# Attention scores that multiply over 128 rows, and token-major products 512 columns wide

## The chip, the core and the metric

The kernel is one program on one core of a Trainium2 chip. The metric is device microseconds of the whole launch; each figure of record is the median of several runs. All data are float32; the program is written in Python for a framework that schedules each engine's queue itself. TensorE does the matrix products, ScalarE and VectorE what lies between them, GpSimd a few elementwise steps, SyncE issues most DMAs.

## What is computed

The reference is three layers on 256 tokens of width 1024. A first block mixes a chunked retention (8 heads) with a gated linear recurrence, and two layers of a second block follow, each with a second sequence of 256 context tokens beside the 256 of x. In such a layer one input projection feeds three branches (an mLSTM, an attention with 8 query and 2 key heads called gqa, an attention with a neighbourhood window and a bias called na); their outputs are projected, gated by sigmoids, summed and multiplied by an output matrix; a feed-forward part with a small convolution closes the layer. Cut to what the change touches:

```python
def attend(q, k, v):                       # gqa, the context tokens
    s = jnp.einsum('bqkgd,bskd->bkgqs', q, k).astype(jnp.float32) * (HEAD_DIM ** -0.5)
    p = jax.nn.softmax(s, axis=-1).astype(v.dtype)
    return jnp.einsum('bkgqs,bskd->bqkgd', p, v)
...
(mq, mk, mv, mo, mg, aq, ak, av, nq, nk, nv, zg) = jnp.split(h @ w_in[l], IN_SPLITS_2, axis=-1)
...
o = merge_branches(y_ml, y_ga, y_na, zg, w_branch[l], w_out[l])
x = x + ga1 * rms_norm_2(o, g_post_mix[l])
f = conv_ffn(modulate(rms_norm_2(x, g_pre_ffn[l]), sh2, sc2), w_up[l], conv_w[l], conv_b[l], w_down[l])
```

The heads of gqa and na are 64 wide. The second layer computes its branches for x alone (its context tokens are needed only as keys and values).

## The kernel before

**Two parts of every operand.** A float32 number goes to TensorE as two float32r parts, high and low. A weight chunk of 128 rows and 1024 columns is loaded (SyncE's queue, four buffers), its high part is a cast on ScalarE (L106), its low part a subtraction on VectorE (L107), or on GpSimd where the call says so. Every product of two such operands is three matmuls: high by high, high by low, low by high (`mm3`, L123 to L125).

**Two forms of product.** Feature-major (`gemm_pieces`, `gemm_feat`): the weights are the stationary operand, 128 by 128, and 256 or 512 tokens move. Token-major (`gemm_tok`, L147): 128 tokens of the activations are stationary and 256 columns of the weights move; both token tiles of a sequence share one PSUM bank of 512 columns, so a call for one sequence holds one bank and a call for two holds two. There are four such banks, named psg in the profile, handed out in turn. A chunk holds four k-tiles of 256 columns. Token-major are the values of the retention (`w_v`), the output projection of the first block (`w_out`), in each layer the queries of gqa (`w_aq`), its keys and values (`w_akv`), the values of mLSTM and na (`w_mv`, `w_nv`), the gate of mLSTM (`w_mo`), the output projection (`w_o`) and the down-projection (`w_dn`, 22 k-tiles). The last two go through `out_proj` (L1129): groups of 256 columns for both sequences, then the last groups for x, the chain of residual and norms of x, and the last groups for the context beside that chain. `take` (L1092) empties a bank: a square with a sum on ScalarE (L1097) and a product with a gate row on VectorE (L1098).

**Scores.** In gqa a query tile holds the high part of a head in rows 0 to 63 and the low part in rows 64 to 127. The keys are kept twice: `akh` has the high part in both halves, so one matmul over 128 rows gives (high + low) of the query by the high part of the key; `akl` has the low part in rows 0 to 63 alone, and a second matmul over 64 rows adds high by low (L838). It writes 256 keys at a time: four matmuls for the 512 keys of x, two for the 256 of the context. na does the same with `nkh` and `nkl`, 512 keys at a time for x (L925); its low parts are made on VectorE (L897) from the bank in which the projection lies.

**Order of the work.** `attend` (L629) walks over units (one head and 128 queries, or one head and two times 128 queries of the context): scores of unit i, then a stretch of other TensorE work that the code calls fillers, then P by V of the pair that closed, then the transposes of unit i-2. Softmax runs meanwhile on VectorE and ScalarE (L657 to L661). The fillers are pieces of the sigmoid gates, of the branch projections and of the conditioning; in gqa a fixed amount is traced with each unit (`FILLS`), in na what is left is spread over the units left. Per layer: 16 units of x in gqa and in na, and in the first layer 8 of the context in each.

## Time and profile before

| | |
|---|---|
| runs | 1889.11, 1892.03, 1887.61 us; median 1889.11 |
| profiled execution: span | 1885.2 us, 31900 instructions |
| its own launch time | not recorded apart from the three runs; the span stands 3.9 us under their median |
| TensorE (matmuls) | busy 1816.7 us, 96% |
| VectorE / ScalarE / GpSimd | 1152.7 / 861.4 / 252.9 us |
| mean granted TensorE clock | 0.987 |

A matmul's end in the profile is modelled and neighbours overlap, so the length of one is not what it costs. What it costs is the step from its start to the start of the next one, which is read in the timeline. "PE" are the matmuls, "PEld" the loads of the stationary operand that run beside them, "DVE" is VectorE, "ACT" ScalarE, "POOL" GpSimd. A form such as 64*128 64x256 says: 64 rows of the array by 128 columns, and 256 moving columns. Clock 1.00 is the upper of TensorE's two levels (2.4 GHz), 0.5 the lower (1.2 GHz).

### The profile page before, as it was taken

The numbers are of one execution on the slowest core, as the hardware profiler recorded it, in microseconds if no ns is written. First come the engines' busy times: TensorE is split into PE (matmuls) and PEld (weight loads), VectorE is DVE, ScalarE is ACT, GpSimd is POOL, SyncE is SP. The second block draws the span as 40 slices with busy tenths as digits, with TensorE's granted clock in tenths as the row PEclk, the third lists the DMA queues.
The fourth block names the chain that finished last, engine by engine and source line by source line (L and its number), as shares of the span: only waits on it lengthen the run. The fifth ranks groups of instructions, "written<-read, shape, count | busy, mean of one in ns | idle before, by whom it ended". The sixth has DMA issues, their size and how long they took to land.

```text
span 1885.2 us, 31900 instructions
## 1 busy us (share of the span) xinstructions
PE 1816.7 (96%) x12484; PEld 1595.4 (85%) x12484; DVE 1152.7 (61%) x2280; ACT 861.4 (46%) x1620; POOL 252.9 (13%) x182
## 2 busy tenths in 40 slices
PE   7998988999999999998999999998999999999998
PEld 6897987666898977787877889998889998779998
DVE  7878768444434667556655564239654448768874
ACT  5463344334435544434444443235555545446653
POOL 2214052000101021004111110021001011002210
PEclk9998998999999999999999999999999999999999
DMA  8853443555524342374354233344444744676563
GB/s 301 282 195 113 138 167 106 184 182 176 193 92 149 88 126 84 101 249 165 113 178 157 96 103 112 107 136 161 151 140 134 239 129 132 196 248 212 185 209 120
DMA packets 114422, 299.33 MB, mean 159 GB/s; under 512 B 28480, under 2 KB 41088, under 8 KB 114016
## 3 DMA queue, kind: packets, MB, share of 16 engines
q1 hardware_dynamic: 113568, 296.37, 47.9%
q8 instruction: 98, 1.61, 0.3%
q0 software_dynamic: 272, 0.36, 0.1%
q10 hardware_dynamic: 432, 0.57, 0.1%
q14 instruction: 52, 0.43, 0.1%
HBM read 281.46 MB, written 19.46 MB: 160 GB/s over the span
## 4 chain that ended last, share of the span: by engine, by line
PE 76%; DVE 6%; ACT 1%; issue 1%; DMA 0%; POOL 0%; DVEq 0%; ACTq 0%; POOLq 0%
PE psg L123 21%; PE psg L124 21%; PE psg L125 20%; PE pss L838 2%; PE psg L692 2%; PE psg L339 2%; PE pst L678 2%; PE pss L925 2%; PE pst L1054 1%; DVE wl L107 1%; PE pss L1042 1%; DVE rstd L240 1%; PE pst L264 0%; ACT wh L106 0%; DVE p L755 0%
## 5 line engine op out<-in xcount | busy, mean ns | idle before, releaser
L107 DVE TENSOR_TENSOR wl<-wr,wh 128x1024 fp32r<-128x1024 f32 x335 | 411.9, 1232 | 328.3 <-ACT wh L106 320.1
L106 ACT CAST wh<-wr 128x1024 fp32r<-128x1024 f32 x370 | 382.4, 1036 | 428.7 <-PE psg L124 182.9
L123 PE MATMUL psg<-hh,wh 128*128 128x256 f32 (+1 forms) x1712 | 577.0, 338 | 0.5 <-ACT hh L279 0.5
L124 PE MATMUL psg<-hl,wh 128*128 128x256 f32 (+1 forms) x1712 | 566.1, 331 | 0.0
L125 PE MATMUL psg<-hh,wl 128*128 128x256 f32 (+1 forms) x1712 | 564.4, 330 | 0.0
L123 PEld LDWEIGHTS psg<-hh,wh 128*128 128x128 f32 x1712 | 327.4, 192 | 54.1 <-issue 16.4
L125 PEld LDWEIGHTS psg<-hh,wl 128*128 128x128 f32 x1712 | 327.8, 192 | 30.2 <-issue 0.8
L124 PEld LDWEIGHTS psg<-hl,wh 128*128 128x128 f32 x1712 | 327.9, 192 | 25.8 <-issue 0.2
L123 PE MATMUL psg<-wh,hh 128*128 128x256 f32 x576 | 165.8, 288 | 6.2 <-DVE p L743 4.3
L125 PE MATMUL psg<-wh,hl 128*128 128x256 f32 x576 | 165.3, 287 | 2.4 <-DVE hl L283 2.4
L124 PE MATMUL psg<-wl,hh 128*128 128x256 f32 x576 | 164.8, 286 | 0.0
L123 PE MATMUL psg<-wh,midh 128*128 128x256 f32 x496 | 140.9, 284 | 0.0
L124 PE MATMUL psg<-wl,midh 128*128 128x256 f32 x496 | 140.9, 284 | 0.0
L125 PE MATMUL psg<-wh,midl 128*128 128x256 f32 x496 | 140.6, 284 | 0.0
L107 POOL TENSOR_TENSOR wl<-wr,wh 128x1024 fp32r<-128x1024 f32 (+1 forms) x35 | 82.5, 2368 | 373.4 <-ACT wh L106 373.4
L1283 POOL TENSOR_TENSOR u<-u 128x512 f32<-128x512 f32 (+1 forms) x44 | 63.3, 1439 | 410.3 <-DVE u L1239 405.3
L123 PEld LDWEIGHTS psg<-wh,hh 128*128 128x128 f32 x576 | 112.1, 195 | 7.1 <-DVE p L743 4.6
L125 PEld LDWEIGHTS psg<-wh,hl 128*128 128x128 f32 x576 | 111.9, 194 | 3.2 <-DVE hl L283 3.2
L124 PEld LDWEIGHTS psg<-wl,hh 128*128 128x128 f32 x576 | 112.0, 195 | 0.1
L123 PEld LDWEIGHTS psg<-wh,midh 128*128 128x128 f32 x496 | 95.6, 193 | 0.0
L124 PEld LDWEIGHTS psg<-wl,midh 128*128 128x128 f32 x496 | 95.6, 193 | 0.0
L125 PEld LDWEIGHTS psg<-wh,midl 128*128 128x128 f32 x496 | 95.6, 193 | 0.0
(300 smaller groups left out, 2915.4 us busy)
## 6 DMA issues: line engine op xcount, KB each, us to landing
wr<-in_w_up_dram SPq DMA_DIRECT2D x88, 512.0 KB, 3.4
wr<-in_w_mod_dram SPq DMA_DIRECT2D x55, 512.0 KB, 3.2
wr<-in_w_zg_dram SPq DMA_DIRECT2D x48, 512.0 KB, 3.5
wr<-in_w_dn_dram SPq DMA_DIRECT2D x45, 512.0 KB, 3.6
wr<-in_w_in_dram SPq DMA_DIRECT2D x40, 512.0 KB, 4.3
wr<-in_w_br_dram SPq DMA_DIRECT2D x24, 512.0 KB, 3.3
wr<-in_w_o_dram SPq DMA_DIRECT2D x20, 512.0 KB, 5.1
stock<-in_w_mod_dram SPq DMA_DIRECT2D x19, 512.0 KB, 6.5
```

The lines of the kernel that those rows point to most:

```text
L106: nc.scalar.copy(hi, raw)
L107: self.last_lo = (eng or nc.vector).tensor_tensor(lo, raw, hi.bitcast(F32), ALU.subtract).ins
L123: mm(ps, a[0], b[0], start=first, stop=False)
L124: mm(ps, a[0], b[1], start=False, stop=False)
L125: mm(ps, a[1], b[0], start=False, stop=last)
L240: nc.vector.scalar_tensor_tensor(w[:, c], t[:, c], t[:, c], v[:, c], ALU.mult, ALU.mult)
L339: nc.tensor.matmul(ps[32 * j : 32 * j + 32, 0:T], self.cv[:, kt], raw[j], start=kt == 0, stop=kt == KT - 1)
L678: nc.tensor.transpose(pt[:, k * P : (k + 1) * P], t[:, k * P : (k + 1) * P], self.idn)
L692: nc.tensor.matmul(po[64 * j : 64 * j + 64, :T], p[2](j, k), pTs[id(p), j][:, k], start=k == 0, stop=k == nk - 1)
L838: nc.tensor.matmul(ps[:, i * T : (i + 1) * T], qT[s, pr][: 64 * (2 - c), j, qt * P : (qt + 1) * P], kT[ss, kv][c], start=c == 0, stop=c == 1)
L925: nc.tensor.matmul(ps[:, :n], q[j][: 64 * (2 - c), s * T + qt * P : s * T + (qt + 1) * P], kk[j][c][:, ks], start=c == 0, stop=c == 1)
L1283: nc.gpsimd.tensor_tensor(a, a, b, ALU.mult)
```

## The change

Two edits in one.

Scores: the low parts of the keys are written into both halves, like the high parts, so the second matmul also runs over 128 rows; it adds the product of both low parts, which the kernel before leaves out. In gqa all 512 keys lie in one tile `akT`, and a unit of x takes two matmuls of 512 columns in place of four of 256.

Products: a new `gemm_wide` takes 512 weight columns at a time, one PSUM bank for each token tile (two banks for one sequence, four for two), two k-tiles a chunk. Before it starts, the piece of other work that is under way is finished. It replaces `gemm_tok` for all token-major products but `w_akv` and the second half of the down-projection's columns. What empties the banks now does it by token tile, 512 columns at a time.

```diff
+    def gemm_wide(self, src, x, seqs, order=None, eng=None, at=None):
+        while self.cur:
+            self.step()
+        pss = {s: [self.bank("g", 4) for _ in range(2)] for s in seqs}
+        nk = src.shape[-1] // 512
+        order = order or list(range(0, nk, 2))
+        for i, k0 in enumerate(order):
+            if at and i in at:
+                at[i]()
+            hi, lo = (a.rearrange("p (k c) -> p k c", c=512) for a in self.weights(src[:, k0 * 512 : (k0 + 2) * 512], eng))
+            for s in seqs:
+                for t in range(2):
+                    for j in range(2):
+                        r = slice(s * T + t * P, s * T + (t + 1) * P)
+                        self.mm3(pss[s][t], x(k0 + j, r), (hi[:, j], lo[:, j]), i + j == 0, i + 1 == len(order) and j == 1)
+        return pss
...
-            for g in range(4):
-                ps = self.gemm_tok(A["w_out"][g], lambda kt, r: (mh[kt // 8][:, kt % 8, r], ml[kt // 8][:, kt % 8, r]), (0,), order=(8, 12, 0, 4))[0]
+            for g in range(2):
+                ps = self.gemm_wide(A["w_out"][g], lambda kt, r: (mh[kt // 8][:, kt % 8, r], ml[kt // 8][:, kt % 8, r]), (0,), order=(8, 10, 12, 14, 0, 2, 4, 6))[0]
...
-                    nc.vector.tensor_tensor(ks[:, :, 2], k, ks[:, :, 0].bitcast(F32), ALU.subtract)
+                    for c in range(2):
+                        nc.vector.tensor_tensor(ks[:, :, 2 + c], k, ks[:, :, c].bitcast(F32), ALU.subtract)
...
-                        kT[s, kv] = [self.tl(gp, [P, T], "akh", 4, F32R), self.tl(gp, [64, T], "akl", 4, F32R)]
-                        nc.scalar.copy(kT[s, kv][0], pt[:, :T])
-                        nc.scalar.copy(kT[s, kv][1], pt[0:64, T:])
+                        nc.scalar.copy(kT[kv][:, :, s * T : (s + 1) * T], pt.rearrange("p (c t) -> p c t", c=2))
...
-                pss = [self.gemm_tok(A[f"w_aq{l}"][g], self.h, (s,), eng=nc.gpsimd if l == 0 else None, among=among if g else None)[s] for g in range(2)]
+                pss = self.gemm_wide(A[f"w_aq{l}"][0], self.h, (s,), eng=nc.gpsimd if l == 0 else None, at=among)[s]
...
-                    for i, ss in enumerate(ks):
-                        for c in range(2):
-                            nc.tensor.matmul(ps[:, i * T : (i + 1) * T], qT[s, pr][: 64 * (2 - c), j, qt * P : (qt + 1) * P], kT[ss, kv][c], start=c == 0, stop=c == 1)
+                    for c in range(2):
+                        nc.tensor.matmul(ps, qT[s, pr][:, j, qt * P : (qt + 1) * P], kT[kv][:, c, s * T : 512], start=c == 0, stop=c == 1)
...
-                    kl = self.tl(pp, [64, 512], "nkl", 4, F32R)
+                    kl = self.tl(pp, [P, 512], "nkl", 4, F32R)
...
-                        nc.scalar.copy(kh[64 * c : 64 * c + 64], src)
-                    nc.vector.tensor_tensor(kl, src, kh[0:64].bitcast(F32), ALU.subtract)
+                        r = slice(64 * c, 64 * c + 64)
+                        nc.scalar.copy(kh[r], src)
+                        nc.vector.tensor_tensor(kl[r], src, kh[r].bitcast(F32), ALU.subtract)
...
-                        nc.tensor.matmul(ps[:, :n], q[j][: 64 * (2 - c), s * T + qt * P : s * T + (qt + 1) * P], kk[j][c][:, ks], start=c == 0, stop=c == 1)
+                        nc.tensor.matmul(ps[:, :n], q[j][:, s * T + qt * P : s * T + (qt + 1) * P], kk[j][c][:, ks], start=c == 0, stop=c == 1)
...
         for t in range(2):
-            nc.scalar.activation(o[:, t, c], ps[:, t], AF.Square, accum_out=ss[:, t, g : g + 1])
-        nc.vector.tensor_tensor(o[:, :, c], ps, G.unsqueeze(1).broadcast_to([P, 2, T]), ALU.mult)
+            p = ps[t] if isinstance(ps, list) else ps[:, t]
+            nc.scalar.activation(o[:, t, c], p, AF.Square, accum_out=ss[:, t, g : g + 1])
+        if isinstance(ps, list):
+            for t in range(2):
+                nc.vector.tensor_tensor(o[:, t, c], ps[t], G, ALU.mult)
...
+            ws = [(A[f"w_dw{l}"][0], 512)] + [(A[f"w_dn{l}"][g], T) for g in range(2)]
```

The values of the retention, `w_mv`, `w_mo`, `w_nv` and `w_o` change in the same way as `w_out`; the weights are laid out for it on the host (`tok(..., 512)`). A new `query_heads` does for the queries, by token tile, what `heads` does by group of four heads. What runs beside the products (the root and the scans of the recurrence, the norm of x) is called at the same fraction of the work as before. `out_proj` has two groups of 512 for `w_o`, and one of 512 and two of 256 for the down-projection.

**TensorE, scores of gqa in the first layer.** Before, a unit of x within the fillers; psg is a bank of a filler, pss the bank of the scores, hh, hl, wh, wl are high and low parts of activations and weights:

```order
L125 MATMUL psg_3932<-hh_109,wl_3912 128x512
L123 MATMUL psg_3932<-hh_109,wh_3911 128x512
L124 MATMUL psg_3932<-hl_110,wh_3911 128x512
L125 MATMUL psg_3932<-hh_109,wl_3912 128x512
L838 MATMUL pss_3951<-akh_3766,aqT_3850 128x256
L838 MATMUL pss_3951<-akl_3767,aqT_3850 128x256
L838 MATMUL pss_3951<-akh_3512,aqT_3850 128x256
L838 MATMUL pss_3951<-akl_3513,aqT_3850 128x256
L123 MATMUL psg_3932<-hh_109,wh_3911 128x512
```

The same place with the change (p is a unit's softmax, which is transposed into pst):

```order
L123 MATMUL psg_3581<-hh_109,wh_3573 128x512
L124 MATMUL psg_3581<-hl_110,wh_3573 128x512
L125 MATMUL psg_3581<-hh_109,wl_3574 128x512
L702 MATMUL pst_3624<-idn,p_3516 128x128 x4
L888 MATMUL pss_3630<-akT_2850,aqT_3453 128x512 x2
L358 MATMUL psg_3411<-wr_3644,cv 32x256 x4
```

Four matmuls of 256 columns, alternating between 128 and 64 rows, are two of 512 columns over 128 rows.

**TensorE, queries of x in the first layer.** Before, the second group of 256 columns (bank psg_3586) begins when the first (psg_3525) is complete, after 48 matmuls:

```order
L124 MATMUL psg_3525<-wl_3559,hh_109 128x256
L125 MATMUL psg_3525<-wh_3558,hl_110 128x256
L123 MATMUL psg_3586<-wh_3589,hh_109 128x256
L124 MATMUL psg_3586<-wl_3590,hh_109 128x256
```

With the change the second token tile (psg_3177) begins after 19 of the 24 matmuls of the first (psg_3176):

```order
L125 MATMUL psg_3176<-wh_3216,hl_110 128x512
L123 MATMUL psg_3176<-wh_3234,hh_109 128x512
L123 MATMUL psg_3177<-wh_3180,hh_109 128x512
L124 MATMUL psg_3177<-wl_3181,hh_109 128x512
L125 MATMUL psg_3177<-wh_3180,hl_110 128x512
```

The second bank, which the queries of the context held before, is asked for after 19 matmuls of 512 columns instead of 48 of 256.

**VectorE, first keys of na in the first layer.** Before, one low part (nkl) for each of two heads around the first unit's bias and maximum:

```order
L897 TENSOR_TENSOR nkl_7059<-psg_7033,nkh_7058 64x512
L928 TENSOR_TENSOR pss_7078<-pss_7078,nbias_6974 128x256
L657 TENSOR_REDUCE sm_7079<-pss_7078 128x1
L897 TENSOR_TENSOR nkl_7064<-psg_7033,nkh_7063 64x512
L658 TENSOR_SCALAR sm_7079<-sm_7079 128x1
```

With the change:

```order
L948 TENSOR_TENSOR nkl_6331<-psg_6305,nkh_6330 64x512 x2
L979 TENSOR_TENSOR pss_6352<-pss_6352,nbias_6246 128x256
L948 TENSOR_TENSOR nkl_6337<-psg_6305,nkh_6336 64x512
L681 TENSOR_REDUCE sm_6353<-pss_6352 128x1
L979 TENSOR_TENSOR pss_6395<-pss_6395,nbias_6246 128x256
L948 TENSOR_TENSOR nkl_6337<-psg_6305,nkh_6336 64x512
```

Each head has two such operations now, the first two of them ahead of the first unit's bias.

## Rows read from the trace of the kernel before

**Rows 1.** The page: busy time of each engine, and the chain that ended last.

```profile
PE 1816.7 (96%) x12484; PEld 1595.4 (85%) x12484; DVE 1152.7 (61%) x2280; ACT 861.4 (46%) x1620; POOL 252.9 (13%) x182
...
PE 76%; DVE 6%; ACT 1%; issue 1%; DMA 0%; POOL 0%; DVEq 0%; ACTq 0%; POOLq 0%
```

**Rows 2.** Stages: PE, PEld, DVE, ACT, POOL busy us (instructions), clock, DMA share, GB/s.

```profile
326.00:470.00 144.00, 144.00 (x830) 99.15 (x830) 62.28 (x134) 54.54 (x118) 0.56 (x1) 1.00 0.53 179
673.00:800.00 127.00, 126.88 (x599) 91.91 (x598) 86.49 (x164) 59.15 (x127) 17.72 (x10) 1.00 0.32 96
1563.00:1632.00 69.00, 68.60 (x445) 50.12 (x443) 57.76 (x121) 38.60 (x76) 11.70 (x10) 1.00 0.52 160
255.00:326.00 71.00, 58.55 (x407) 53.34 (x405) 59.76 (x141) 33.83 (x65) 28.07 (x23) 0.88 0.36 124
1298.00:1332.00 34.00, 29.39 (x224) 27.85 (x222) 28.57 (x77) 20.27 (x46) 8.11 (x13) 0.95 0.35 116
```

**Rows 3.** Timeline of PE, scores of one gqa unit: start, length, operation.

```profile
420.95 0.36 PE L838 MATMUL pss<-akh,aqT 128*128 128x256 f32 x1
...
422.18 0.42 PE L339 MATMUL psg<-wr,cv 128*32 128x256 f32 x4
```

**Rows 4.** Timeline of PE, scores of two na units, with what follows each.

```profile
680.39 0.39 PE L925 MATMUL pss<-nkh,nq 128*128 128x512 f32 x1
...
681.13 0.50 PE L123 MATMUL psg<-hh,wh 128*128 128x512 f32 x1
...
685.68 0.48 PE L925 MATMUL pss<-nkh,nq 128*128 128x512 f32 x1
...
686.52 0.50 PE L123 MATMUL psg<-yh,wh 128*128 128x512 f32 x1
```

**Rows 5.** Timeline of PE, first and last of 57 token-major matmuls of 256 columns.

```profile
299.73 0.28 PE L125 MATMUL psg<-wh,hl 128*128 128x256 f32 x1
...
306.45 0.28 PE L124 MATMUL psg<-wl,hh 128*128 128x256 f32 x1
```

**Rows 6.** Timeline of PE, first and last of nine feature-major matmuls of 512 columns.

```profile
417.60 0.39 PE L125 MATMUL psg<-hh,wl 128*128 128x512 f32 x1
...
419.42 0.39 PE L124 MATMUL psg<-hl,wh 128*128 128x512 f32 x1
```

**Rows 7.** Groups by form on PE and PEld: count, busy us, mean ns, idle before.

```profile
L123 PE MATMUL psg<-wh,hh 128*128 128x256 f32 x576 | 165.8, 288 | 6.2 <-DVE p L743 4.3 <-ACT fs L288 1.7
L123 PE MATMUL psg<-wh,midh 128*128 128x256 f32 x496 | 140.9, 284 | 0.0
L123 PE MATMUL psg<-wh,mgh 128*128 128x256 f32 x192 | 54.3, 283 | 0.0
L123 PE MATMUL psg<-wh,mh 128*128 128x256 f32 x128 | 36.0, 282 | 0.0
L838 PE MATMUL pss<-akl,aqT 64*128 64x256 f32 x80 | 30.2, 380 | 0.0
L925 PE MATMUL pss<-nkl,nq 64*128 64x512 f32 x32 | 15.7, 495 | 0.0
L925 PE MATMUL pss<-nkl,nq 64*128 64x256 f32 x16 | 6.1, 380 | 0.0
L123 PEld LDWEIGHTS psg<-wh,hh 128*128 128x128 f32 x576 | 112.1, 195 | 7.1 <-DVE p L743 4.6 <-ACT fs L288 1.9 <-ACT hh L282 0.3
```

**Rows 8.** Groups by form on ACT and DVE that the change lengthens or repeats.

```profile
L735 ACT ACTIVATE p<-psg 128x512 f32<-128x512 f32 x6 | 3.4, 598 | 0.9 <-DVE u L253 0.9
L1098 DVE TENSOR_TENSOR o<-psg,fs 128x512 f32<-128x512 f32 x23 | 15.9, 691 | 29.8 <-ACT o L1097 29.8
L897 DVE TENSOR_TENSOR nkl<-psg,nkh 64x512 fp32r<-64x512 f32 x16 | 11.0, 686 | 1.3 <-ACT nkh L896 1.0
L772 DVE TENSOR_TENSOR hs<-p,hs 128x256 fp32r<-128x256 f32 x4 | 1.7, 415 | 0.5 <-ACT hs L771 0.5
```

**Rows 9.** Timeline of PE, first matmul of the second group of the queries of x.

```profile
295.14 0.58 PE L123 MATMUL psg<-wh,hh 128*128 128x256 f32 x1 [4.33 <-DVE p L743]
```

More of the change, by code (lines that the diff above doesn't have):

```diff
@@ L757, in heads, with query_heads @@
                     yield v3(t1)
-            kT, vt, qT = {}, {}, {}
+            def query_heads(pss):
+                s, pss = pss
+                v3 = lambda a: a.rearrange("p (h f) -> p h f", f=64)
+                r = self.tl(gp, [P, 16], "hss", 2)
+                for t, ps in enumerate(pss):
+                    sq = self.tl(gp, [P, 512], "p", 5)
+                    nc.scalar.activation(sq, ps, AF.Square)
+                    nc.vector.tensor_reduce(r[:, 8 * t : 8 * t + 8], v3(sq), AX.X, ALU.add)
+                self.rstd(gp, r, r, 64)
+                for t, ps in enumerate(pss):
+                    qn = self.tl(gp, [P, 512], "p", 5)
+                    nc.vector.tensor_tensor(v3(qn), v3(ps), r[:, 8 * t : 8 * t + 8].unsqueeze(2).broadcast_to([P, 8, 64]), ALU.mult)
+                    if s == 1:
+                        nc.vector.tensor_tensor(v3(qn), v3(qn), gq.unsqueeze(1).broadcast_to([P, 8, 64]), ALU.mult)
+                        yield v3(qn)
+                        continue
+                    t1 = self.tl(gp, [P, 512], "p", 5)
+                    t2 = self.tl(gp, [P, 512], "p", 5)
+                    over = lambda c: c.unsqueeze(1).broadcast_to([P, 8, c.shape[-1]])
+                    nc.gpsimd.tensor_tensor(v3(t1), v3(qn), over(rot[0][:, 0, t]), ALU.mult)
+                    for a in range(4):
+                        q, o = 16 * (a ^ 1), 16 * a
+                        nc.vector.tensor_tensor(v3(t2)[:, :, o : o + 16], v3(qn)[:, :, q : q + 16], over(rot[0][:, 1, t, o : o + 16]), ALU.mult)
+                    nc.vector.tensor_tensor(t1, t1, t2, ALU.add)
+                    yield v3(t1)
+            vt, qT = {}, {}
+            kT = [self.tl(gp, [P, 2, 512], "akT", 2, F32R) for _ in range(2)]
             def keys(qs):
@@ L821, in gqa @@
             if l == 0:
-                k1, q1, k0, q0 = keys((1,)), queries(1, (1, lambda: next(put(self.yx, 0)))), keys((0,)), queries(0)
+                k1, q1, k0, q0 = keys((1,)), queries(1, {3: lambda: next(put(self.yx, 0))}), keys((0,)), queries(0)
                 order = (k1, q1, k0, behind(k1), q1, k1, q0, k0, q1, q0, k0, fill(fills[0]), q0)
@@ L1203, in layer @@
             o = {s: self.tl(pp, [P, 2, D], f"o{s}") for s in qs}
[L1204 removed]
+            ss = {s: self.tl(pp, [P, 2, 2], f"oss{s}") for s in qs}
             self.new_h()
@@ L1213, in post, with take @@
                 return ys
-            def take(ps, s, g):
-                self.take(ps, o[s], ss[s], l, 0, s, g)
-                self.fetch([w for w in late if not w.loaded][:3])
+            def take(ps, s, g, c):
+                self.take(ps, o[s], ss[s], l, 0, s, g, c)
+                self.fetch([w for w in late if not w.loaded][: 6 if l else 3])
             n = {}
             self.out_proj(
-                A[f"w_o{l}"],
+                [(A[f"w_o{l}"][g], 512) for g in range(2)],
                 lambda kt, r: (mh[:, kt, r], ml[:, kt, r]),
```

128 lines of the change are left out of this document (66 added, 62 removed).

## Prediction

> **What bounds the kernel now.** I read the page first: the matmuls keep TensorE busy for 96% of the span, and the chain that ended last runs for 76% of it through TensorE [rows 1]. The table by stage then tells where that holds. In the gqa stage of the first layer, and in the na stage of both, TensorE has no free time, while VectorE is busy for 62 of 144, 86 of 127 and 58 of 69 us [rows 2]. At the two places where a layer's gqa begins it is otherwise: TensorE is busy for 58.6 of 71 and 29.4 of 34 us, VectorE for 59.8 and 28.6 [rows 2], and the work there is a chain of norms and rotations. So a shorter matmul is worth its full size in the attention units and in the long products, and little at those two starts.
>
> Last, the timeline of TensorE, for the steps from start to start. Token-major matmuls of 256 columns step by 6.72/56 = 0.120 us [rows 5], matmuls of 512 columns by 1.82/8 = 0.2275 us [rows 6]. Both use all 128 rows, and the load of the stationary operand, 0.195 us long [rows 7], is hidden beside the matmul before. The scores don't step like that: four of 256 columns take 422.18 - 420.95 = 1.23 us, 0.3075 each [rows 3], and a pair of 512 columns takes 0.74 to 0.84 us [rows 4] where two plain steps would be 0.455. What sets them apart is that every second one uses 64 rows [rows 7]. A change from 128 to 64 rows, or back, costs 0.19 us a time, about the length of one load.
>
> **Scores over 128 rows.** In gqa there are 160 score matmuls (80 with 64 rows [rows 7], as many with 128), which is 40 fours: 40 x 1.23 = 49.2 us. Afterwards the 32 fours that belong to x are two matmuls of 512 columns, 32 x 0.455 = 14.6 us, and the 8 of the context four plain ones of 256, 8 x 0.48 = 3.8 us: 18.4 in all, a gain of 30.8. In na there are 32 pairs of 512 columns and 16 of 256 [rows 7]. At the mean of the two pairs seen, 0.79 us, and at half a four, 0.615 us, they take 25.3 + 9.8 = 35.1 us; afterwards 32 x 0.455 + 16 x 0.24 = 18.4. Gain 16.7. Together 47.5 us, all inside stages where TensorE is the bound.
>
> Added for it: the second low part of the na keys, 16 operations on VectorE of 0.686 us, and of the gqa keys, four of 0.415 us [rows 8]. The casts of the keys lose as many as they gain. In the second layer's na stage this meets VectorE: 57.8 us of work there becomes 57.8 + 8 x 0.686 = 63.3, while TensorE's 68.6 loses about a third of 16.7, some 5.6, and comes to 63.0. Two engines that both need 63 us won't overlap fully. At best the stage ends after 63.3 us and nothing is lost; at worst VectorE keeps all its idle time, 11 us, and the stage takes 74.5, a loss of 11. I take 3 off, nearer the first end, because VectorE waits there on work that TensorE now delivers sooner. In the first layer's na, VectorE comes to 92 of about 116 us and stays covered. At the head of each na stage one more of these operations stands ahead of the first unit's bias: 2 x 0.686 = 1.4 us off.
>
> **Products of 512 columns.** The first of three matmuls stands 576 + 496 + 192 + 128 times in the four large token-major groups [rows 7], and 32 times in the last product of all. Unchanged are 64 for the gqa keys (two layers, two sequences, two token tiles, eight k-tiles) and half of the down-projection's 528. That leaves 512 + 264 + 192 + 128 = 1096, times three, 3288 matmuls, which become 1644 of double width. Each pair gains 2 x 0.120 - 0.2275 = 0.0125 us: 20.6 us. The same bytes arrive in the same 1024-column chunks, and one chunk feeds the same time of matmuls, so loads, casts and low parts keep their cover.
>
> Not all of it counts. The queries' 144 pairs (96 and 48 in the two layers) lie in the starts that VectorE bounds: 1.8 us off, and 1.7 more for the four extra low parts of the gqa keys, which stand in VectorE's chain there. The context's part of the first layer's output projection runs beside the chain of norms of x, which sets the end: 48 pairs, 0.6 us off. At the first start, the second bank of the queries of x is now asked for after 19 x 0.2275 = 4.3 us instead of 48 x 0.120 = 5.8, so the wait of 4.33 us seen there [rows 9] can grow by 1.4. I count none of it: VectorE's chain, not the end of these matmuls, sets the end of that stretch; 1.4 is the upper end. Emptying a bank of 512 columns takes 0.60 us on ScalarE and 0.69 on VectorE [rows 8] for a token tile. The first tile of the last chunk closes six matmuls, 1.4 us, before the second, so its emptying hides beside them; nothing is counted either way.
>
> **The sum.** 47.5 + 20.6 - 3.0 - 1.4 - 1.8 - 1.7 - 0.6 = 59.6 us. The profiled execution's span of 1885.2 becomes 1825.6; the median of the runs stands 3.9 us above that span, which gives 1829.5, rounded to 1830 us.
>
> **Rivals.** (a) The fixed part of a step is not paid per matmul. Rows 5 and 6 come from different operands, and the 512-column step was seen for feature-major products alone. If the wide token-major matmul took two narrow steps, 0.240 us, the 18.2 us counted for the products would be gone: 1848. For it is only that no wide token-major matmul exists yet; against it, that the same columns of the same type go through the same rows. The Trainium skill ("TensorE: Matmul & The Clock Gate", Back-to-back issue gap) gives a step of columns over 2.4 GHz plus 2.5 ns; by that the pairs would gain an estimated 1644 x 0.0025 = 4.1 us and the time would be about 1844. The steps in the trace leave 13 ns over the columns at either width, so here the trace decides against that figure.
>
> (b) Loads stay exposed, and filling the rows does nothing. If a load waited for the matmul before it whatever the rows, the scores would step by 0.2275 + 0.195 and 0.120 + 0.195. gqa would then take 64 x 0.4225 + 32 x 0.315 = 37.1 us, na the same, and the gain of 47.5 shrinks to 49.2 + 35.1 - 74.2 = 10.1: 1867. The same page (The mechanism) says that a load overlaps a matmul only where their row groups differ, which speaks for this case and against the change. Rows 5 contradict it: a load of 0.195 us can't lie outside a step of 0.120.
>
> (c) Softmax becomes the bound. If the shorter units wait on VectorE and ScalarE and half the gain of the scores is lost, the time is 1854. For it speaks the na stage of the second layer; against it the gqa stage, where VectorE is idle for 82 of 144 us [rows 2].
>
> (d) The banks. A wide product of two sequences holds all four psg banks, one of one sequence two, so the next product can wait for a reader at each of the 20 wide calls. With the wait of 4.33 us [rows 9] at every one it costs 87 us: 1917, slower. It cancels the gain from 3.0 us a call on. Against it: the four tiles of the last chunk close 1.4 us apart, and a reader takes 0.6 or 0.7 us [rows 8]; the one wait seen comes from a chain of norms between the product and the reader, which the other calls don't have.
>
> **How the numbers follow.** The forecast gets 0.81, rival (a) 0.06, (b) 0.03, (c) 0.05, (d) 0.03, and 0.02 is for a time below the range. Under the forecast the known ends are 1821, where nothing is lost (68.1 us), and 1840, where the na stage loses 11 in place of 3 and the bank wait its 1.4, rounded up. I go down to 1816, since some of TensorE's 12 free us in the first start may close, and up to 1849 to take in rival (a). A measurement of this kernel can tell about 0.2%, 3.8 us, from no change. All cases but (d) are faster by far more: faster 0.96; a mild (d) gives no change 0.01 and the rest slower 0.03.
>
> **What would show it.** TensorE should have 1708 fewer matmuls (1644 + 64): 10776. The score matmuls and those that follow them should step by 0.2275 and 0.120 with no 0.19 us extra; wide token-major ones by 0.2275. The gqa stage of the first layer should shrink by about 18 us, the second layer's by about 12, the first na stage by 11, the second by only 2 to 3 with VectorE above 90%. The two starts should keep their lengths. The forecast is wrong if wide matmuls step by 0.24, if scores keep steps of 0.3 or more, or if new waits for banks appear at the wide products.

## The result, and the profile after

The changed kernel takes 1828.55 us (median of 4 runs, 1827.0 to 1829.88) against 1888.36 for the kernel before (1885.93 to 1892.03) on the same chip: ratio 0.9682, 95% interval 0.9666 to 0.9699. The forecast was 1830. The profiled execution spans 1825.2 us where the one before spanned 1885.2.

The line of the page on the engines, to be held against [rows 1]:

```profile
PE 1750.8 (96%) x10776; PEld 1491.0 (82%) x10776; DVE 1157.2 (63%) x2288; ACT 857.8 (47%) x1562; POOL 251.3 (14%) x182
```

There are 10776 matmuls, the number forecast, and TensorE's share of the span is what it was. The stages of the kernel after, with the columns of [rows 2]: gqa of the first layer from its first score to its last product with V, na of the first and of the second layer, and the two starts of gqa up to the first score. The windows of [rows 2] are not cut at the same places; the lengths of the same stages before stand in the table of the next section.

```profile
323.00:465.30 142.30, 142.30 (x892) 102.15 (x890) 67.72 (x145) 60.33 (x127) 1.08 (x2) 1.00 0.64 211
650.70:766.80 116.10, 115.94 (x609) 90.85 (x608) 90.50 (x171) 59.93 (x127) 17.86 (x10) 1.00 0.33 100
1508.10:1580.00 71.90, 66.08 (x455) 51.37 (x455) 60.95 (x128) 38.31 (x75) 13.43 (x10) 1.00 0.48 154
249.00:323.00 74.00, 59.25 (x317) 48.24 (x316) 60.38 (x138) 33.47 (x60) 29.36 (x23) 0.91 0.39 124
1240.40:1290.40 50.00, 44.60 (x313) 41.50 (x311) 45.41 (x122) 30.48 (x61) 7.52 (x13) 0.97 0.43 130
```

The second na stage before, from its first score to its last product with V:

```profile
1563.80:1635.90 72.10, 71.26 (x465) 52.47 (x466) 57.95 (x122) 38.41 (x75) 11.70 (x10) 1.00 0.49 154
```

There TensorE now waits: it is idle for 5.8 of 71.9 us, where it was idle for 0.8 of 72.1, while VectorE went from 58 to 61 us.

The loads show what the scores did. Before, the PEld timeline of one gqa unit (start, length, operation; the matmuls of this unit are [rows 3]):

```profile
420.92 0.19 PEld L838 LDWEIGHTS pss<-akh,aqT 128*128 128x128 f32 x1
421.24 0.18 PEld L838 LDWEIGHTS pss<-akl,aqT 64*128 64x128 f32 x1
421.55 0.19 PEld L838 LDWEIGHTS pss<-akh,aqT 128*128 128x128 f32 x1
421.86 0.18 PEld L838 LDWEIGHTS pss<-akl,aqT 64*128 64x128 f32 x1
```

After, the matmuls of a unit with the one behind it, then the loads of the same stretch:

```profile
401.65 0.70 PE L888 MATMUL pss<-akT,aqT 128*128 128x512 f32 x2
402.19 0.39 PE L123 MATMUL psg<-hh,wh 128*128 128x512 f32 x1
402.41 0.39 PE L124 MATMUL psg<-hl,wh 128*128 128x512 f32 x1
...
401.62 0.30 PEld L888 LDWEIGHTS pss<-akT,aqT 128*128 128x128 f32 x2
401.96 0.19 PEld L123 LDWEIGHTS psg<-hh,wh 128*128 128x128 f32 x1
402.19 0.19 PEld L124 LDWEIGHTS psg<-hl,wh 128*128 128x128 f32 x1
```

Before, a load and its own matmul start together (the second to fourth matmul of this unit start at 421.24, 421.55 and 421.87), and a step of 0.31 us is a plain step of 0.12 [rows 5] and the 0.19 us of a load: the load lies open. After, the second score matmul starts at 401.96; the load for the matmul of 402.19 begins with it and is hidden. Two score matmuls and the step to the next take 0.54 us instead of 1.23.

The first and the last of 15 wide token-major matmuls in the down-projection:

```profile
1114.69 0.39 PE L124 MATMUL psg<-wl,midh 128*128 128x512 f32 x1
...
1117.86 0.39 PE L123 MATMUL psg<-wh,midh 128*128 128x512 f32 x1
```

They step by 3.17/14 = 0.2264 us, close to the 0.2275 of the feature-major ones [rows 6]. Rival (a) falls with that. The step is 13 ns above 512 columns at 2.4 GHz (213.3 ns). The Trainium skill ("TensorE: Matmul & The Clock Gate", Back-to-back issue gap) gives 2.5 ns above the columns, for an isolated matmul; in this trace, with a load for each matmul, it is 13 ns.

### The profile page after: what moved, and what is told of

It reads as the page before. It is cut to its first block, busy times and chain, and to the rows that moved or that the text cites. A ratio compares the mean times of both kernels' runs of the same rounds, so it can differ in the third digit from the quotient of the medians.

```text
span 1825.2 us, 28352 instructions
## 1 busy us (share of the span) xinstructions
PE 1750.8 (96%) x10776; PEld 1491.0 (82%) x10776; DVE 1157.2 (63%) x2288; ACT 857.8 (47%) x1562; POOL 251.3 (14%) x182
## 5 line engine op out<-in xcount | busy, mean ns | idle before, releaser
L107 DVE TENSOR_TENSOR wl<-wr,wh 128x1024 fp32r<-128x1024 f32 (+1 forms) x333 | 412.0, 1239 | 350.2 <-ACT wh L106 343.0
L123 PEld LDWEIGHTS psg<-hh,wh 128*128 128x128 f32 x1712 | 326.8, 191 | 46.9 <-issue 11.5
L123 PE MATMUL psg<-wh,hh 128*128 128x512 f32 (+1 forms) x320 | 120.6, 377 | 7.4 <-DVE p L767 5.3
L125 PE MATMUL psg<-wh,hl 128*128 128x512 f32 (+1 forms) x320 | 119.9, 375 | 2.1 <-DVE hl L302 2.1
L124 PE MATMUL psg<-wl,hh 128*128 128x512 f32 (+1 forms) x320 | 119.7, 374 | 0.0
L123 PE MATMUL psg<-wh,midh 128*128 128x256 f32 (+1 forms) x364 | 117.7, 323 | 0.0
L124 PE MATMUL psg<-wl,midh 128*128 128x256 f32 (+1 forms) x364 | 117.6, 323 | 0.0
L125 PE MATMUL psg<-wh,midl 128*128 128x256 f32 (+1 forms) x364 | 117.4, 322 | 0.0
L123 PEld LDWEIGHTS psg<-wh,hh 128*128 128x128 f32 x320 | 61.2, 191 | 17.9 <-DVE p L767 5.5
L683 ACT ACTIVATE p<-pss,sm 128x512 f32<-128x512 f32 x64 | 44.0, 687 | 63.7 <-DVE sm L682 63.5
L125 PEld LDWEIGHTS psg<-wh,hl 128*128 128x128 f32 x320 | 61.2, 191 | 12.5 <-DVE hl L302 2.5
```

What stands on the lines that cost most here:

```text
L107: self.last_lo = (eng or nc.vector).tensor_tensor(lo, raw, hi.bitcast(F32), ALU.subtract).ins
L123: mm(ps, a[0], b[0], start=first, stop=False)
L124: mm(ps, a[0], b[1], start=False, stop=False)
L125: mm(ps, a[1], b[0], start=False, stop=last)
L683: nc.scalar.activation(t, s, AF.Exp, bias=m, accum_out=z)
```

## The experiments

The table gives the length of each stretch in the profiled execution, in us, worked out from the starts of its first and last matmuls. The last two columns are the first two experiments.

| stretch | before | change | scores alone | products alone |
|---|---|---|---|---|
| `w_v` and `w_out` | 75.2 | 71.1 | 75.2 | 71.1 |
| first start of gqa, to the first score | 71.4 | 74.0 | 69.3 | 74.2 |
| first gqa, to its last P by V | 160.2 | 142.3 | 143.3 | 159.5 |
| from there to the first score of na | 187.9 | 185.5 | 189.2 | 184.1 |
| first na | 129.9 | 116.0 | 116.0 | 129.9 |
| first `w_o` | 46.0 | 43.3 | 46.0 | 43.3 |
| first down-projection | 134.4 | 131.4 | 135.2 | 131.6 |
| second start of gqa | 46.9 | 50.0 | 50.1 | 45.4 |
| second gqa | 93.6 | 78.6 | 78.6 | 93.4 |
| from there to the first score of na | 140.9 | 139.1 | 142.2 | 137.8 |
| second na | 72.1 | 71.9 | 71.5 | 71.7 |
| second `w_o` | 23.9 | 21.6 | 24.3 | 21.7 |
| last product and end | 70.8 | 69.3 | 70.8 | 69.3 |

One stretch moves by itself: the first start takes 72.5 us in the run with the rows grouped (below), whose code there is that of the kernel before, which took 71.4.

### Each edit by itself

**Scores alone**, the kernel before with the edits of `keys`, `score` and na's `prepare`, of which the last:

```diff
-                    kl = self.tl(pp, [64, 512], "nkl", 4, F32R)
+                    kl = self.tl(pp, [P, 512], "nkl", 4, F32R)
```

> The kernel before with the scores edit alone. By the prediction's terms: 47.5 gained on TensorE, less 3.0 (VectorE in the second na stage), 1.4 (heads of the na stages) and 1.7 (low parts of the gqa keys) = 41.4 us, so 1888.4 - 41.4 = 1847 us. First gqa stage (first score to last P by V) -17 to -18 us, first na stage -13 to -14, second na stage 0 to -3. If the two edits are worth only together what they gave (a gain in one exposes the other's), this run and the one with the products alone sum to less than 57 or to more than 62 us. The starts of gqa: if the added low parts of the keys lengthen them, both starts grow here as they did with the change (2.6 and 3.1 us up to the first score); if the wide queries do, they keep their lengths here.

Measured: 1847.35 us against 1887.47, ratio 0.9794 (0.9777 to 0.981), a gain of 40.1 where 41.4 stood. The first gqa and the two na stages change by -16.9, -13.9 and -0.6 us, about as expected. The starts do neither of the two things written there: the first is 2.1 us shorter, the second 3.2 longer.

**Products alone**, the changed kernel with those edits undone:

```diff
-                    for c in range(2):
-                        nc.tensor.matmul(ps, qT[s, pr][:, j, qt * P : (qt + 1) * P], kT[kv][:, c, s * T : 512], start=c == 0, stop=c == 1)
+                    for i, ss in enumerate(ks):
+                        for c in range(2):
+                            nc.tensor.matmul(ps[:, i * T : (i + 1) * T], qT[s, pr][: 64 * (2 - c), j, qt * P : (qt + 1) * P], kT[ss, kv][c], start=c == 0, stop=c == 1)
```

> The changed kernel with the scores of before. By the prediction's terms 20.6 - 1.8 - 0.6 = 18.2 us gained: 1870 us; w_out -2.5, w_o -2.7 and -2.3, down-projection of the first layer -3.0 as with both edits. If the fixed part of a step were not paid per matmul (rival a), the wide products would gain under 2 us: 1887 or more. The starts of gqa: if the wide queries lengthen them, they grow here by up to 2.6 and 3.1 us; if the low parts of the keys do, they keep their lengths here.

Measured: 1866.97 us, ratio 0.9893 (0.9878 to 0.9908), a gain of 20.5 where 18.2 stood. The gains sum to 60.6 us, the change itself gave 59.8: they add. Each long product shortens by the same amount in the run with products alone as in the change, and by about what stood there (`w_o` by 2.7 and 2.2 us, the first down-projection by 2.8). The first start is 2.8 us longer, the second 1.5 shorter.

### What the 64 rows cost

**Rows grouped**, the kernel before with another order within a four:

```diff
-                        for c in range(2):
-                            nc.tensor.matmul(ps[:, i * T : (i + 1) * T], qT[s, pr][: 64 * (2 - c), j, qt * P : (qt + 1) * P], kT[ss, kv][c], start=c == 0, stop=c == 1)
+                        for n, c in enumerate((0, 1) if i == 0 else (1, 0)):
+                            nc.tensor.matmul(ps[:, i * T : (i + 1) * T], qT[s, pr][: 64 * (2 - c), j, qt * P : (qt + 1) * P], kT[ss, kv][c], start=n == 0, stop=n == 1)
```

> The kernel before, with the four score matmuls of a unit of x in gqa in the order 128, 64, 64, 128 rows in place of 128, 64, 128, 64: the same eighty matmuls over 64 rows, but two changes of rows a unit fewer. Theory (each change costs 0.19 us): 32 units x 2 x 0.19 = 12.2 us gained, 1876 us; the step between the two 64-row matmuls is 0.12 us. Rival (each matmul over 64 rows, or each load for one, costs the extra 0.38 us whatever stands beside it): no change, 1888.

**Narrow scores over 128 rows**, the changed kernel with the 512 keys in two halves:

```diff
-                    for c in range(2):
-                        nc.tensor.matmul(ps, qT[s, pr][:, j, qt * P : (qt + 1) * P], kT[kv][:, c, s * T : 512], start=c == 0, stop=c == 1)
+                    for i in range(s, 2):
+                        for c in range(2):
+                            nc.tensor.matmul(ps[:, (i - s) * T : (i - s + 1) * T], qT[s, pr][:, j, qt * P : (qt + 1) * P], kT[kv][:, c, i * T : (i + 1) * T], start=c == 0, stop=c == 1)
```

> The changed kernel, with four score matmuls of 256 columns per unit of x in gqa in place of two of 512, all over 128 rows. Theory (the change of rows was the cost): 32 units x (4 x 0.120 - 2 x 0.2275) = 0.8 us slower than the change, 1829 to 1830 us, and the steps inside a four are 0.12 us. Rival (the number of score matmuls and loads was the cost, the rows nothing): the fours go back to about 1.2 us each, 32 x 0.75 = 24 us slower, 1852; if rows and width share the gain, about 1841. If the first score of before could begin earlier because it needed the keys of x alone, the span up to the first score shrinks again by up to 1.9 us in the second layer, with no gain at the end.

Measured: the grouped order 1873.41 us, ratio 0.9934 (0.9913 to 0.9955), that is 8 to 16 us gained where 12 stood; the two gqa stages shrink by 5.3 and 5.4 us. The narrow scores over 128 rows 1826.9 us, ratio 0.9683 (0.9669 to 0.9698), the same as the change. So the rows were the cost; neither the width nor the number of score matmuls was.

The timelines give the size. In the first layer eleven units of x are followed by three matmuls of 512 columns (ten in the kernel before). From the first score matmul to the start of the third of these, the median is

| | changes of rows | us |
|---|---|---|
| before (128, 64, 128, 64) | 4 | 1.802 |
| grouped (128, 64, 64, 128) | 2 | 1.417 |
| four of 256 columns over 128 rows | 0 | 1.018 |
| two of 512 columns over 128 rows | 0 | 1.025 |

Two changes fewer are worth 0.385 us and the other two 0.399: 0.19 to 0.20 each. That is the mean of the two directions, since each order has as many changes from 128 rows to 64 as back. One thing of the expectation failed: the step from one 64-row matmul to the next was 0.223 us in the median, where 0.120 stood. The record of a matmul whose load is not hidden starts with its load, so that load lies in the step behind it. In the grouped order the two 64-row matmuls, the next one, and the loads of the two:

```profile
404.12 0.50 PE L838 MATMUL pss<-akl,aqT 64*128 64x256 f32 x2
404.56 0.39 PE L838 MATMUL pss<-akh,aqT 128*128 128x256 f32 x1
...
404.12 0.29 PEld L838 LDWEIGHTS pss<-akl,aqT 64*128 64x128 f32 x2
```

The two loads, 0.18 us each, take 0.29 us together: the second does not wait for the first matmul to end. The steps of a four can't be priced one by one, their sum can.

The narrow scores also settle the second start. It is 46.9 us long again, with 80.7 for the gqa stage behind it. The wide first matmul of a unit needs the keys of both sequences; the narrow one starts as soon as those of x are there. So 3.1 us of the 50.0 are a mark that moved, and all but about 1.2 of them return in the stage: from the end of the down-projection to the first maximum of the softmax the change takes 50.7 us, the kernel before 49.5.

### What took the gain in the second na stage

**Low rows of the na keys zero**, the changed kernel with:

```diff
+            kls = [self.tl(pp, [P, 512], f"nkl{i}", 1, F32R) for i in range(4)]
+            for kl in kls:
+                nc.gpsimd.memset(kl[64:128].bitcast(F32), 0.0)
...
-                        nc.vector.tensor_tensor(kl[r], src, kh[r].bitcast(F32), ALU.subtract)
+                    nc.vector.tensor_tensor(kl[0:64], src, kh[0:64].bitcast(F32), ALU.subtract)
```

> The changed kernel; the low parts of the na keys are written to rows 0 to 63 alone, as before, and rows 64 to 127 of four fixed tiles are set to zero by GpSimd once a layer. The matmuls still use 128 rows; left out is the product of both low parts, as in the kernel before. Eight operations of 0.686 us on VectorE go from the second na stage, sixteen from the first. Theory (VectorE's queue ends the waits in the second na stage): its new waits go, the stage shrinks from 71.9 by 3 to 5 us, VectorE's busy time there from 61 to 55.5; the first na stage, bounded by TensorE, changes by under 1. Total 3 to 6 us below the changed kernel: 1823 to 1826 us. Rival (the units are too short for the round trip from score to softmax and back, whatever VectorE's load): the stage stays within 1 us, 1828 us.

Measured: 1823.97 us, ratio 0.9655 (0.9642 to 0.9668). What TensorE waits for in the second na stage (us in total, times, longest), first in the kernel before:

```profile
PE psg L692 <- DVE pT L681: 0.6, 1, 0.6
PE pss L925 <- ACT nkh L896: 0.2, 1, 0.2
PE psg L692 <- ACT pT L683: 0.2, 1, 0.2
```

In the changed kernel:

```profile
PE pss L976 <- ACT p L683: 3.1, 3, 1.3
PE psg L123 <- DVE fs L1222: 1.7, 2, 1.4
PE psg L716 <- ACT pT L707: 0.7, 1, 0.7
PE psg L716 <- DVE pT L705: 0.3, 1, 0.3
```

Then with the rows zeroed, and behind it the stage as in the windows above:

```profile
PE pss L978 <- ACT p L683: 0.7, 1, 0.7
PE pst L702 <- DVE sm L682: 0.6, 1, 0.6
PE psg L716 <- DVE pT L705: 0.3, 1, 0.3
PE pss L978 <- ACT nkh L949: 0.2, 1, 0.2
PE psg L716 <- ACT pT L707: 0.2, 1, 0.2
...
1507.90:1576.50 68.60, 66.81 (x465) 52.82 (x466) 56.95 (x121) 38.40 (x75) 12.62 (x10) 1.00 0.52 162
```

The waits fall from 5.8 to 2.0 us and the stage by 3.2, with eight operations of VectorE fewer: the second low parts took the gain. The heads of both na stages, counted in the stretch ahead, shrink by 1.4 us each. But the first score comes earlier with them, so that more fillers stand behind it (ten matmuls more in the second stage), and the first na stage takes 117.1 us instead of 116.0, where a change of under 1 stood. Head and stage together, the second low parts cost 0.3 us at the first na and 4.6 at the second.

### What lengthened the starts

**Low rows of the gqa keys zero**, the changed kernel with:

```diff
+            for k in kT:
+                nc.gpsimd.memset(k[64:128, 1].bitcast(F32), 0.0)
...
-                    for c in range(2):
-                        nc.vector.tensor_tensor(ks[:, :, 2 + c], k, ks[:, :, c].bitcast(F32), ALU.subtract)
+                    nc.vector.tensor_tensor(ks[:, :, 2], k, ks[:, :, 0].bitcast(F32), ALU.subtract)
```

> The changed kernel; the low parts of the gqa keys are made once and lie in rows 0 to 63 of a tile whose rows 64 to 127 are set to zero once a layer by GpSimd; the product of both low parts is left out, as before. Four operations on VectorE go (two at each layer's start of gqa). Theory (the start of the second layer really lost 1.2 us, counted up to the first maximum, and the second low parts with the weights' low part that now stands ahead of them are its cause): that start shrinks by 0.7 to 1.2 us, the first layer's by 0 to 0.7; 1827 to 1829 us. Rival (VectorE's chain there doesn't end the wait): nothing at either start.

Measured: 1826.95 us, ratio 0.967 (0.9657 to 0.9683), which the intervals don't tell from the change. The second start is 1.9 us shorter, and the stage behind it 1.6 longer; the first start keeps its length. The second low parts of the gqa keys cost no more than the noise.

**Narrow queries**, the changed kernel with:

```diff
-                pss = self.gemm_wide(A[f"w_aq{l}"][0], self.h, (s,), eng=nc.gpsimd if l == 0 else None, at=among)[s]
+                pss = [self.gemm_tok(A[f"w_aq{l}"][g], self.h, (s,), eng=nc.gpsimd if l == 0 else None, among=among if g else None)[s] for g in range(2)]
...
-                for q in query_heads((s, pss)):
+                for q in heads(pss, 4, (s, s), 0):
```

> The changed kernel with the queries of gqa as before: two groups of 256 columns, and the heads by groups of four. It has 144 x 2 matmuls of 256 columns in place of 144 of 512, 1.8 us more of TensorE's work in the two starts. Theory (the wide queries lengthen the first layer's start, since the run with products alone had it 2.8 us longer and the one with scores alone 2.0 shorter): that start falls from 74.0 to 69 to 72 us; the second layer's grows by up to 1.5, which the products alone took off. Total -3 to +0.5 us against the changed kernel: 1825 to 1829. Rival (another wide product or the order of the banks lengthens the start): it stays at 74 and the 1.8 us are added, 1830.

Measured: 1830.75 us, ratio 0.9691 (0.9678 to 0.9704), above what stood there. The first start falls to 72.4 us, but the stage behind it takes 144.2 instead of 142.3. The mark has moved again: eight of the queries' transposes stand behind the first score here, and ahead of it in the change. From the end of `w_out` to the last P by V it is 216.6 us, against 216.3 in the change and 212.7 with the scores alone. The width of the queries is not the cause.

The trace shows a cause that was not on the list. In the first start of the changed kernel, GpSimd makes low parts of weights, and VectorE the chain that normalises the keys of the context. Timeline of GpSimd, then of VectorE, then of TensorE's wait for the chain, the one that answers to [rows 9]:

```profile
280.21 4.88 POOL L107 TENSOR_TENSOR wl<-wr,wh 128x1024 fp32r<-128x1024 f32 x2 [3.86 <-ACT wh L106]
285.91 2.34 POOL L107 TENSOR_TENSOR wl<-wr,wh 128x1024 fp32r<-128x1024 f32 x1 [0.82 <-ACT wh L106]
...
282.77 0.41 DVE L760 TENSOR_REDUCE hss<-p 128x4 f32<-128x256 f32 x1
283.21 1.91 DVE L247 TENSOR_SCALAR rstd<-hss 128x4 f32<-128x4 f32 x1
285.15 0.17 DVE L248 TENSOR_SCALAR rstd<-rstd 128x4 int32<-128x4 int32 x1
...
285.95 2.31 DVE L255 SCALAR_TENSOR_TENSOR rstd<-rstd,rstd 128x4 f32<-128x4 f32 x1
...
289.48 0.49 DVE L767 TENSOR_TENSOR p<-psg,hss 128x128 f32<-128x128 f32 x2
...
290.02 0.80 PE L123 MATMUL psg<-wh,hh 128*128 128x512 f32 x1 [5.31 <-DVE p L767]
290.61 0.63 PE L124 MATMUL psg<-wl,hh 128*128 128x512 f32 x1
```

Operations on four columns take 0.17 us, but 1.91 and 2.31 when GpSimd is at work, and they end where its operation ends (285.12 and 288.26 against 285.09 and 288.25). Not every operation is held: the reduction of 0.41 us ahead of them runs inside the same GpSimd operation. Nor are only the smallest: the low part `hl` of 256 columns, 0.41 us by itself, takes 2.4 to 2.6 us at three places of this start. Behind the wait the first matmuls of 512 columns step by 0.43 to 0.59 us; the stretch has a granted clock of 0.91. The Trainium skill ("SBUF — State Buffer", SBUF: two separate sides) says that VectorE and GpSimd share a pair of ports: of a GpSimd operation and a VectorE operation with two inputs in SBUF, or in a mode that uses both ports, the one that starts first holds the pair for its whole instruction and blocks the other. These rows agree, but the trace does not tell an operation's mode.

**First start with its low parts on VectorE**, the changed kernel with, in `keys` and `queries`:

```diff
-, eng=nc.gpsimd if l == 0 else None
```

> The changed kernel; at the first layer's start of gqa the low parts of the weights of queries, keys and values, twelve operations of 2.4 us on GpSimd, are made by VectorE (1.2 us each). Theory (a small operation on VectorE that meets one on GpSimd lasts until that is over, so the chain of norms loses some 2.2 us at each meeting, and the first layer's start moved by 2 us only because the meetings fall otherwise): the rows of 1.4 to 2.5 us among VectorE's small operations go, some 10 us before the keys are normed; VectorE takes 8 to 10 operations of 1.2 us in that stretch in exchange, those of them that fall into its waits for nothing. The start shrinks from 74.0 to 66 to 73 us; total 1821 to 1828. Rival (the small operations are long for another reason, such as the table of their first use): the long rows stay, VectorE's added work lengthens the start by 5 to 10 us.

Measured: 1814.86 us, ratio 0.9612 (0.9599 to 0.9626), 13 us below the change run beside it and better than expected. The same places, VectorE and then TensorE:

```profile
276.19 0.17 DVE L247 TENSOR_SCALAR rstd<-hss 128x4 f32<-128x4 f32 x1
...
277.20 0.16 DVE L255 SCALAR_TENSOR_TENSOR rstd<-rstd,rstd 128x4 f32<-128x4 f32 x1
...
278.57 0.49 DVE L767 TENSOR_TENSOR p<-psg,hss 128x128 f32<-128x128 f32 x2
...
279.12 0.50 PE L123 MATMUL psg<-wh,hh 128*128 128x512 f32 x1 [1.42 <-DVE p L767]
279.45 0.39 PE L124 MATMUL psg<-wl,hh 128*128 128x512 f32 x1
...
249.00:310.50 61.50, 54.94 (x318) 44.54 (x318) 53.64 (x149) 34.11 (x60) 7.62 (x13) 1.00 0.45 143
```

No long row is left, the first start takes 61.5 us instead of 74.0, and TensorE holds its upper clock level through it. Of the 12.5 us, 8.2 are idle time of TensorE (14.8 to 6.6 us); the other 4.3 are its busy time (59.3 to 54.9), at a granted clock of 1.00 instead of 0.91, which the expectation left out. TensorE did not wait for the slower low parts of GpSimd themselves: its waits of over 1 us in the first start of the change (5.3, 4.8, 1.9 and 1.5 us) are all for VectorE. From the end of `w_out` to the norm of the context's keys it is 29.5 us, against 40.5 in the change. The same mark stands at 40.3 before, at 40.6 with the products alone and at 38.1 with the scores alone; that last one has one meeting fewer among its norms (four long rows, five before; the six of the change last about as long together as those five, 11.7 and 11.3 us). This accounts for 2 us between the runs' first starts. The second half of that start takes 33.5 us with the wide products, where it took 31.1 before. About 1 us of that goes with the clock: the run with the rows grouped has the code of before there, and where TensorE's wait is 5.3 us instead of 4.3, its second half takes 32.2 us, at a granted clock of 0.90 instead of 0.93. The rest stays open; the queries' width alone isn't it.

### A version that beats both

Beside the last run ran the changed kernel once more, and the zeroed rows of both kinds of keys together (the two diffs above).

> The changed kernel itself, beside the two others on the same chip: 1828 to 1829 us.

Measured: 1827.9 us, ratio 0.9683 (0.967 to 0.9696).

> The zeroed rows of the na keys and of the gqa keys together. If the two gains add: 4.5 from na, 0 to 1.5 from gqa (its own run was within a few us of the change), so 1822.5 to 1824 us. Rival (what the gqa keys save is given back in the stage behind, as in the run with them alone): 1824, like the na rows alone.

Measured: 1820.43 us, ratio 0.9641 (0.9628 to 0.9654), 2 us better than expected. In its first start one meeting is missing, so that is 3.6 us shorter. Then the zeroed rows together with the first start's low parts on VectorE:

> The zeroed rows of the na and gqa keys and the first layer's gqa start with its low parts on VectorE, together. By the runs alone: 1828 - 7.5 - 13 = 1807.5 us, if they add. Part of what the zeroed rows showed in the first start (3.6 us) came from one meeting less between VectorE and GpSimd, and there are none left here to save, so 1807.5 to 1811; the start is 61 to 62 us.

Measured: 1812.04 us, ratio 0.9602 (0.9588 to 0.9616), by the ratios some 2 us better than VectorE's low parts alone, and just above the expected range. That the first start's 3.6 us can't be had twice was in the range (the start is 61.4 us); the 1 us beyond it stays open. Last, the other low parts that GpSimd makes beside a chain of norms:

```diff
-            put(gemm(w, x, (1,), eng=self.nc.gpsimd, **among)[1], 1, g, cs)
+            put(gemm(w, x, (1,), **among)[1], 1, g, cs)
...
-                    ws = [up_w(i, nc.gpsimd), up_w(22 + i, nc.gpsimd)]
+                    ws = [up_w(i), up_w(22 + i)]
```

> The same, and the low parts of the output and down-projection's last products for the context and of the first up-projection weights on VectorE as well. Theory (meetings with GpSimd): in the first layer's chain of norms behind the output projection, small operations of 1.4, 2.3 and 2.3 us become 0.17, so TensorE's wait there of 8.3 us shrinks by up to 5.4 us, less VectorE's own low parts in front of the chain (up to three of 1.2 us); behind the down-projection there is a wait of 3.9 us that can shrink by up to 2. Total 1 to 7 us below the other run. Rival (the low parts in front of the chain cost VectorE as much as the meetings): within 1 us, or slower by up to 3.

Measured: 1797.32 us, ratio 0.9526 (0.9512 to 0.9539), 14.7 us below the other run where 1 to 7 stood. In the changed kernel the chain behind the first `w_o` had these rows (VectorE, then TensorE):

```profile
839.23 2.26 DVE L248 TENSOR_SCALAR rstd<-rstd 128x2 int32<-128x2 int32 x1
841.52 2.27 DVE L249 TENSOR_SCALAR rstd<-rstd 128x2 int32<-128x2 int32 x1
...
845.99 0.47 PE L283 MATMUL pst<-idn,o 128*128 128x128 f32 x1 [8.29 <-DVE o L272]
```

Without them on GpSimd (nine low parts in the first block stay there):

```profile
822.55 0.17 DVE L248 TENSOR_SCALAR rstd<-rstd 128x2 int32<-128x2 int32 x1
822.75 0.17 DVE L249 TENSOR_SCALAR rstd<-rstd 128x2 int32<-128x2 int32 x1
...
826.76 0.44 PE L283 MATMUL pst<-idn,o 128*128 128x128 f32 x2 [0.65 <-DVE o L272]
```

TensorE's wait goes from 8.29 us (8.31 in the run that this one is compared with) to 0.65, and the stretch from the last matmul of `w_o` to the transposes from 10.1 to 3.3. The first down-projection falls from 130.9 to 125.2: its wait of 3.90 us for the chain becomes 0.61, and most of the other 2.4 us are matmuls and transposes that step shorter, at a granted clock of 1.00 over the last 25 us instead of 0.94 over the last 28. The expectation left out the clock, and two long rows more: in the run compared with, operations of 2.42 and 2.32 us stand in the same chain ahead of the three that it counted, before the last matmul of `w_o`.

## Why the prediction was right

The sum of 59.6 us was met by 59.8, with terms that miss by a few us and cancel in part; so close a meeting is luck. The mechanism was right: the price of a change of rows and the step of a wide matmul came out as forecast.

- **Price of a change of rows.** 0.19 us was forecast, 0.19 to 0.20 measured. In gqa the fours were priced from the first score to the next matmul [rows 3], which missed two things of about 0.1 us each: a load that still lies open behind the transposes (the new pair and the step to the next matmul take 0.54 us, not 0.455), and the excess on the matmul behind a four, which went too (0.337 to 0.233 us). They cancel: 1.802 - 1.025 = 0.78 us a unit, forecast 0.775.
- **First gqa stage:** forecast -18, measured -18.0. **Second:** forecast about -12, measured -14.9 with 3.1 on the start ahead, together -11.8.
- **First na stage:** forecast -11, measured -13.9. The term "the mean of the two pairs seen, 0.79 us" left out the matmul behind a pair, and "32 x 0.455" the load behind the transposes, where a score matmul of 512 columns steps by 0.315 us. The steps of the score matmuls there sum to 22.8 us before and 13.0 after; those of the 512-column products to 86.2 (359 of them) and 82.1 (352). Seven products that now lie elsewhere are 1.6 us of these 4.1, and the other 2.5 are the excess behind a change.
- **Second na stage:** forecast -2 to -3 with VectorE above 90%, measured -0.2 with 60.95 of 71.9 us, 85%. The eight added operations cost 3.2 us there, as the run without them shows, so the 3 us taken off for them were about right. The step that failed is the term beside it, that TensorE "loses about a third of 16.7, some 5.6": even without those operations the stage ends only 3.4 us sooner than before (68.7 against 72.1). The steps of the score matmuls there sum to 12.8 us before and to 9.2 without the operations, where plain steps would be 7.3: behind the transposes a load still lies open. TensorE also waits 2.0 us in that stage, where it waited 1.0 before. The added operations did not fill VectorE's idle time either, as 85% shows; without them TensorE waits 3.8 us less, so their place in VectorE's queue cost more than their sum.
- **Heads of the na stages:** the 1.4 us counted for both are 1.4 each, but at the first na 1.1 of them come back in the stage. Heads and stages together cost 4.9 us (0.3 and 4.6), where the sum had 1.4 + 3.0: the total was right, its places were not. A key's second cast on ScalarE now waits for the low part ahead of it (1.40 us at the head of the second na stage), which the count of operations left out.
- **Products.** 20.6 us gross and 18.2 net were forecast; 20.5 were measured. The step of a wide matmul is the one forecast, or a little under it (0.2264 by 0.2275: 22 us for all pairs). What was taken off for the queries was not lost at the second start, but the first start took 2.8 us; that the two meet at 20.5 is luck. Nothing shows the 1.7 us taken off for the second low parts of the gqa keys: the run without them can't be told from the change.
- **The two starts** "should keep their lengths": they are 2.6 and 3.1 us longer up to the first score. At the second one most is the mark that moved. At the first the chain on VectorE does set the end, as was said, but the rows were misread. The wait of [rows 9] is that of the first group of the queries of x, not of the second (96 matmuls follow it), for the bank of the context's keys. It grew from 4.33 to 5.31 us because TensorE arrives earlier at a chain that ends where it did, not because a bank is asked for sooner. The same wait is 5.32 us in the run with the rows grouped, which has the narrow products of before there, so not even the growth can be put down to the change.
- **Rivals.** (a) fell with the step of 0.2264 us. (b) fell with the narrow scores over 128 rows: inside a four they step by 0.118 us in the median, less than a load's 0.19. (c) shows in the second na stage alone. (d) did not come: in the whole trace one wide product waits for a bank for more than 1 us, the one that [rows 9] answer to.

## What to carry to other kernels

Read the price of a matmul from the step to the next one, and go on to the matmul behind the group, since an open load shows in a later step. If a small operand fills half of the rows, fill the rest, with zeros where that saves work elsewhere: 128 rows all along hid the loads behind matmuls of 256 and 512 columns, though not behind transposes of 128 columns, where about 0.09 us stayed open (0.315 us for a step instead of 0.2275); the zeros cost a few writes per layer. Look for small VectorE operations that last as long as a GpSimd one: in the first start VectorE was busy for 60.4 us with GpSimd making low parts beside it, and for 53.6 when it made them itself.

## What was not expected of the hardware

- A VectorE operation on two or four columns lasts up to 2.4 us instead of 0.17 when it meets a 2.4 us operation on GpSimd, and ends with it; a reduction beside the same operation kept its 0.41 us. Moving 12 such GpSimd operations to VectorE, where each takes 1.2 us, gained 13 us at one place.
- A change between 64 and 128 rows cost 0.19 to 0.20 us, on the mean of both directions, and of two 64-row matmuls behind one another only the changes around them cost extra.
